# Modulation row sums issued beside the attention, single PSUM banks for the paired products, attention results fetched one load earlier, and program order kept on two engines in all pairs

## The chip, the cores and the metric

The kernel runs on one core of a Trainium2 chip. The metric is the device time of one execution in microseconds (us), lower is better. The program's instructions run on TensorE (PE), VectorE (DVE), ScalarE (ACT) and GpSimd (POOL); SyncE (SP) issues most of the transfers between HBM and the on-chip memory. Each engine works through its own instructions in the order in which they stand in its list, and waits for the others by semaphores.

## What is computed

One layer, in fp32, over 512 prompt tokens and 64 sample tokens (576 in all, width 1024): a modulation vector from the condition `c`, a normalised and modulated input, one wide projection, a gated causal convolution beside a sliding-window attention with sinks (16 heads of 64, 4 key heads, window 128), their gated mix, and then a gated feed-forward with its own causal convolution.

```python
mod = jax.nn.silu(c) @ w_ada + b_ada
sh1, sc1, g1, sh2, sc2, g2 = [m[:, None, :] for m in jnp.split(mod, 6, axis=-1)]
h = _rmsnorm(x, norm1_g) * (1.0 + sc1) + sh1
proj = h @ w_in
b_gate, c_gate, xa, q, k, v, ga, gb = jnp.split(proj, cuts, axis=-1)
uc, new_conv = _causal_conv(c_gate * xa, conv_buf, conv_w)
ya = (b_gate * uc) @ w_conv_out
o, k_state, v_state = attend(q, k, v, attn_sinks.reshape(N_KV_HEADS, GROUP))
yb = o @ w_attn_out
mixed = jax.nn.sigmoid(ga) * ya + jax.nn.sigmoid(gb) * yb
x = x + g1 * (mixed @ w_mix_out)
h2 = _rmsnorm(x, norm2_g) * (1.0 + sc2) + sh2
...
```

The sample tokens attend to cached keys and values. Of `mod`, columns 0 to 2047 (sh1, sc1) are needed at the start; columns 2048 to 6143 (g1, sh2, sc2, g2) only behind the attention. The outputs are both normalised token streams and the new convolution, key, value and feed-forward states.

## The kernel before

**Products.** An fp32 product is made from three matmul passes over operands split in a high and a low part (`whi`, `wlo` of a weight, `hh`, `hl` and the like of the input). The splits, made on ACT and DVE, are what these two engines mostly do. Two output blocks of 128 rows by 576 tokens are computed as a pair (`pair_product`) from seven part products of 288 columns instead of eight. A part is 12 matmuls into one of three PSUM banks X, Y and Z. The order is X, Z, Y, X, Y, Z, Y. Behind a part another engine reads its bank: ACT subtracts X into Y (behind part 1), copies Z to `p` (part 2) and subtracts Y into Z (part 3); DVE or the result's own function reads X (part 4), Y with `p` (part 5), Z with `p` (part 6) and Y (part 7).

**Banks.** PSUM has two pools here: `mm`, two tiles of 1024 columns, and `aux`, four banks of 512 that serve everything else in turn. In pairs 0 to 13 (`N_ATT` is 14) X and Y are in two `mm` tiles and Z in an `aux` bank; later X and Z are in `aux`, Y in `mm`.

**Jobs.** The wide projection and the convolution's output product run as 27 pairs, in the loop over `jobs` near the end of the kernel: gates, queries, convolution inputs and gates (0 to 22), then `w_conv_out` (23 to 26). Products with `w_attn_out`, `w_mix_out`, `w_up` and `w_down` follow.

**Work beside them.** A generator set by `fill` is stepped from `tick(2)`, once in each part behind its third matmul, at a rate of steps per tick. Beside the pairs it first yields the attention, 16 units of one key head and one block of 128 tokens. A unit's scores (`prompt_scores`), mask (`s<-V,aux`), maximum (`nmx`), exponentials, sums (`den`) and scaling are written out in one step; transposes (`prompt_turn`) and values (`prompt_values`) come in later steps. The decode steps follow, then `modulation(2048)`, which loads 32 tiles of 128 x 512 of `w_ada` (`ada`, 256 KB each, on SP's queue) and sums them in 8 calls of `side_by_side` (8 matmuls, 32 rows each, into four row groups of one bank). `modulation(4096)` is stepped beside the last job and the attn_out products.

**What sets the order.** A scheduler may move instructions, but not those issued through `pe`, `act`, `dve` and `pool` while they are in the list `pinned`: `keep_in_program_order` then puts such an instruction behind the one that was written out just before it on its engine. PE is pinned throughout; `act` and `dve` are added when pair 14 is reached. The attention's own ACT and DVE instructions are issued through `nc.scalar` and `nc.vector` and are not pinned themselves. Weight loads (`raw`, four buffers) and `ada` loads share SP's queue; a weight load waits there until its buffer is free.

**Attention results.** The outputs are written to `ot_dram`. `load_o` fetches them as `or` tiles and `part_o` splits them (`oh` first, on ACT) for the attn_out products: in the last job's steps two are loaded at step 0, and each `part_o(n)` loads up to `n + 2`.

Of the kernel before, what the change touches and what calls it, by code (L numbers as in the profile page):

```python
# [27 lines left out]
FCH = [(0, 8), (8, 22)]  # L28
FB = 14
LATE = 2  # L30
ROWS_AHEAD = 5
N_ATT = 14
Q_TICKS = 8
OPS_AT = 1, 2, 3, 4
CACHE_AT = 17
# [39 lines left out]
def step_kernel(ctx: ExitStack, tc: tile.TileContext, ins: dict, outs: list):  # L75
# [9 lines left out]

    cnt = [0]

    pm = ctx.enter_context(tc.tile_pool(name="pm", bufs=2, space=PSUM))
    pa = ctx.enter_context(tc.tile_pool(name="pa", bufs=4, space=PSUM))

    def nm(s):
        cnt[0] += 1
# [6 lines left out]
        return ap_.tile([P, 594], F32, tag="uy", name=nm(s), bufs=U_BUFS)  # L99

    def mmps():
        return pm.tile([P, 1024], F32, tag="mm", name=nm("mm"))

    def aux():
        return pa.tile([P, 512], F32, tag="aux", name=nm("aux"))
# [374 lines left out]
        order = {0: "sums1 ah al", 2: "bh bl sums2", 3: "dh dl", c_at: "ch cl"}  # L480
        return {at: (lambda names=names: [t[n]() for n in names.split()]) for at, names in order.items()}

    def pair_product(w, x, steps, out_a0, out_a1, out_b0, out_b1, apart=False, scale=1.0):

        X, Y = (halves(mmps())[1][:, :HT] if apart or n else aux()[:, :HT] for n in range(2))
        Z = aux()[:, :HT]
# [594 lines left out]
    def decode_values(q, s, cV):  # L1083
        pt = []
        for kt in range(2):
            a = aux()
            for hd in range(4):
                transpose(
                    a[:, hd * P : hd * P + P], s[hd // 2][:, hd % 2, kt * P : kt * P + P], ident
                )  # L1090
            t = slot("pt", shape=[P, 512])
            nc.scalar.copy(t, a)
            pt.append(t)
            yield False
        yield False
        c = slice(32 * q, 32 * q + 32)
        if not od:
            od.append(slot("od", shape=[P, NK, 64]))
        for j in range(2):
            O = aux()  # L1100
            parts = [(vt(4)[:, j * P : j * P + P], pt[1], slice(0, P))]
            for b in range(4):
                parts.append((cV[b // 2][:, b % 2, j * P : j * P + P], pt[0], slice(32 * b, 32 * b + 32)))
            for n, (v, x, r) in enumerate(parts):
                for hf in range(2):
                    at = (2 * j + hf) * P
                    matmul(
                        O[HALF[hf], r], v[:, HALF[hf]], x[:, at + r.start : at + r.stop],
                        start=n == 0, stop=n == 4,
                    )  # L1110
            oX = slot("oX", shape=[P, 2, 32])
            for hf in range(2):
                src = O[HALF[hf], :P].rearrange("p (b x g t) -> p x g b t", b=4, x=2, g=2)
                dst = od[0][:, 4 * j + 2 * hf : 4 * j + 2 * hf + 2, c]
                nc.scalar.copy(
                    dst[HALF[hf]].rearrange("p g (b t) -> p g b t", b=4), src[:, hf]
                )
                nc.scalar.copy(
                    oX[HALF[hf]].rearrange("p g (b t) -> p g b t", b=4), src[:, 1 - hf]
                )  # L1120
                nc.sync.dma_start(dst[HALF[1 - hf]], oX[HALF[hf]])
            yield False
# [58 lines left out]
                if i == 3:  # L1181
                    nc.scalar.dma_start(ot_dram[2 * hd + g], ot[2 * hd + g])

    def attention():
        units = [(hd, i) for hd in range(4) for i in range(4)]
        s, pts = {}, {}
        for n in range(len(units) + 3):
            if n == CACHE_AT:
                cache_load(0)
            if n < len(units):  # L1190
                hd, i = units[n]
                while 2 * hd + 1 not in QS or ticks[0] < ready[hd]:
                    yield False
                s[n] = prompt_scores(hd, i)
            if n >= 4 and n % 2 == 0:
                prompt_values([(*units[u], pts.pop(u)) for u in (n - 4, n - 3)])
            yield False
            if 2 <= n <= len(units) + 1:
                pts[n - 2] = prompt_turn(units[n - 2][1], s.pop(n - 2))
            yield False  # L1200
        filler[1] = .45
        before = None
        for n in range(3):
            s, more = [], []
            if n < 2:
                yield from decode_scores(n, s, more)
            if before is not None:
                yield from before
            before = decode_values(n, s, more)
# [52 lines left out]
    def side_by_side(ps, ks, cols):  # L1262
# [2 lines left out]
        order = [(k, j) for k in reversed(ks) for j in (3, 0, 1, 2)]  # L1265
        for n, (k, j) in enumerate(order):
            done = nc.tensor.matmul(  # L1267
                ps[32 * j : 32 * j + 32, :], cT[:, k, :], cols[k][j],
                start=(k == 1), stop=(k == NK - 2),
            )  # L1270
            if n:
                tc.keep_in_program_order(done)

    def modulation(c0):

        ps = aux()
        cols = [[None] * 4 for _ in range(NK)]
        for n in range(4 * NK + ROWS_AHEAD):
            if n < 4 * NK:
                k, j = n // 4, n % 4  # L1280
                cols[k][j] = slot("ada", shape=[P, 512])
                c = c0 + 512 * j
                nc.sync.dma_start(cols[k][j], ins["w_ada"][0, k * P : k * P + P, c : c + 512])
            yield False
            done = n + 1 - ROWS_AHEAD
            if done > 0 and done % 8 == 0:
                side_by_side(ps, (done // 4 - 2, done // 4 - 1), cols)
                yield False
        row = slot("row", shape=[P, 512])
        nc.scalar.copy(row, ps)  # L1290
        yield False
        t = aux()
        yield False
        for cc in range(4):
            transpose(t[:, cc * P : cc * P + P], row[:, cc * P : cc * P + P], ident)
        b0 = c0 // P
        nc.vector.tensor_tensor(
            out=modT[:, b0 : b0 + 16, :].rearrange("p (j c) r -> p j c r", j=4),
            in0=t.rearrange("p (c j r) -> p j c r", c=4, j=4)[:, :, :, 0:9],
            in1=parT[:, b0 : b0 + 16]  # L1300
            .rearrange("p (j c) -> p j c", j=4)
            .unsqueeze(3)
            .to_broadcast([P, 4, 4, 9]),
            op=ALU.add,
        )
        yield False

    def modulations(n):
        yield from modulation((2048, 4096)[n])
        yield True  # L1310

    def beside_conv():
        yield from attention()
        filler[1] = 40 / 84
        yield from modulation(2048)
        yield True

    fill(beside_conv(), .28)
# [214 lines left out]
    for n in range(4):  # L1533
        if n:
            jobs[n_conv + n].before = {
                1: [lambda n=n: late[2 * n - 2]()], 2: [lambda n=n: late[2 * n - 1]()],
            }
    jobs[-1].after = {
        0: [lambda: load_o(2)], 2: [lambda: part_o(2)], 3: [lambda: part_o(3)],
        4: [lambda: w_next.update({1: split_w(w_raw)})], 5: [lambda: part_o(4)], 6: [lambda: part_o(6)],  # L1540
        7: [lambda: part_o(8)],
    }
# [9 lines left out]
    def part_o(n):  # L1552
        for k in range(len(o), n):
            o.append(split_slot(o_raw[k], "o"))
        load_o(min(n + 2, NK))

    for n, job in enumerate(jobs):
        if n == N_ATT:
            pinned += [act, dve]
        if n + 1 == len(jobs):  # L1560
            drain()
            fill(modulations(1), 0.6)
        if n + 2 < len(jobs):
            jobs[n + 2].load()
        elif n + 2 > len(jobs):
# [5 lines left out]
        pair_product(job.w, job.ops["op"], joined(job.before, steps, job.after), *outs, n < N_ATT, job.scale)  # L1571
# [701 lines left out]
```

## Time and profile before

| | |
|---|---|
| time, median of 3 runs | 974.13 us (972.2 to 977.55) |
| the profiled execution | 974.38 us |
| its span, first to last instruction | 972.6 us |
| mean granted PE clock | 0.991 |
| POOL busy | 142.5 us (15%) |
| HBM traffic over the span | 134 GB/s |

In rows of the profile a line such as `PE L117 MATMUL aux<-t,whi` names the engine, the line of the kernel (often that of the helper that issues all pinned instructions: 117 in before, 136 in the changed kernel), the operation, and the tile written and the ones read. `x2` counts instructions that are merged in one row. In brackets stands the idle time ahead of the instruction and what ended it. Busy time of PE counts its matmuls. The pairs run from about 73 us on; the attention's units lie between 74 and 270 us, the modulations between 339 and 470 us.

### The profile page before, as it was taken

How to read it: one execution, taken by the hardware profiler on the slowest of the kernel's cores; microseconds unless marked ns; L12 is line 12 of the kernel's file. 1: busy time of each engine (PE TensorE's matmuls, PEld its weight loads, DVE VectorE, ACT ScalarE, POOL GpSimd, SP SyncE). 2: the span in 40 equal slices, each digit the busy share in tenths (PEclk: the TensorE clock that was granted, in tenths of full speed). 3: DMA queues.
4: the chain of work that ended last, by engine and by line, in shares of the span. 5: the costliest groups of instructions: out<-in, count | busy, mean ns of one | idle time of the engine just before them, and what ended most of it. 6: DMA issues, size and time to landing. Idle time of an engine off the chain costs nothing.

```text
span 972.6 us, 18634 instructions
## 1 busy us (share of the span) xinstructions
PE 944.0 (97%) x7218; PEld 900.2 (93%) x7218; DVE 723.5 (74%) x1366; ACT 572.3 (59%) x1086; POOL 142.5 (15%) x320
## 2 busy tenths in 40 slices
PE   7999999999999999897999999999999999999997
PEld 6798989988999989797899999999999999999997
DVE  5687987879586676665677678995558998868874
ACT  5366777767667656675445657564226655546664
POOL 2221111022121222111000121100000000001110
PEclk9999999999999999898999999999999999999999
DMA  9976466544565999789895742233333333327542
GB/s 287 315 219 178 113 197 170 158 110 110 157 167 137 235 254 275 206 223 280 271 280 163 170 116 73 66 108 88 86 89 96 99 88 87 104 65 175 136 95 98
DMA packets 186442, 154.30 MB, mean 159 GB/s; under 512 B 7896, under 2 KB 162332, under 8 KB 186066
## 3 DMA queue, kind: packets, MB, share of 16 engines
q1 hardware_dynamic: 173698, 113.81, 39.1%
q0 software_dynamic: 11360, 36.94, 17.5%
q10 hardware_dynamic: 1296, 2.36, 0.7%
q8 instruction: 56, 0.92, 0.4%
q14 instruction: 32, 0.26, 0.1%
HBM read 115.98 MB, written 14.17 MB: 134 GB/s over the span
## 4 chain that ended last, share of the span: by engine, by line
PE 82%; DMA 7%; ACT 5%; DVE 2%; issue 2%; SPq 1%; POOL 0%; ACTq 0%; DVEq 0%; POOLq 0%
PE mm L117 46%; PE aux L117 34%; DMA ada<-in_w_ada 2%; PE aux L1267 2%; ACT whi L117 1%; DMA ad<-in_w_ada 1%; DMA wlo<-raw 1%; PE aux L1169 1%; DMA or<-ot_dram 1%; ACT s L1009 1%; DMA raw<-in_w_in 1%; DMA raw<-in_w_down 1%; ACT wlo L117 1%; SPq L531 1%; DMA out<-so 0%
## 5 line engine op out<-in xcount | busy, mean ns | idle before, releaser
L117 ACT ACTIVATE whi<-raw 128x1024 fp32r<-128x1024 f32 (+3 forms) x192 | 194.7, 1023 | 112.1 <-PE aux L117 35.4
L117 DVE TENSOR_TENSOR wlo<-raw,whi 128x1024 fp32r<-128x1024 f32 (+3 forms) x153 | 180.2, 1184 | 29.8 <-ACT whi L117 29.5
L117 DVE TENSOR_TENSOR raw<-raw 128x512 f32<-128x512 f32 x100 | 70.1, 701 | 2.4
L117 PE MATMUL aux<-2h,whi 128*128 128x288 f32 (+2 forms) x232 | 68.7, 296 | 0.0
L117 PE MATMUL aux<-2h,wlo 128*128 128x288 f32 (+2 forms) x232 | 68.5, 295 | 0.0
L117 PE MATMUL aux<-2l,whi 128*128 128x288 f32 (+2 forms) x232 | 68.5, 295 | 0.0
L117 POOL DMA_DIRECT2D wlo<-raw x39 | 34.4, 881 | 184.4 <-ACT wlo L117 69.8
L117 PE MATMUL aux<-hh,whi 128*128 128x288 f32 (+2 forms) x180 | 53.2, 303 | 0.0
L117 PE MATMUL aux<-hh,wlo 128*128 128x288 f32 (+2 forms) x180 | 51.9, 295 | 0.0
L117 PE MATMUL aux<-hl,whi 128*128 128x288 f32 (+2 forms) x180 | 51.8, 295 | 0.0
L117 PE MATMUL mm<-fh,whi 128*128 128x256 f32 x224 | 47.8, 295 | 0.3 <-DVE rt L117 0.3
L117 PE MATMUL mm<-fh,wlo 128*128 128x256 f32 x224 | 47.7, 295 | 0.0
L117 PE MATMUL mm<-fl,whi 128*128 128x256 f32 x224 | 47.1, 292 | 0.0
L117 PE MATMUL mm<-hh,whi 128*128 128x288 f32 (+2 forms) x160 | 45.3, 307 | 0.5 <-ACT hh L117 0.5
L117 PEld LDWEIGHTS aux<-2h,whi 128*128 128x128 f32 x232 | 43.6, 188 | 0.0
L117 PEld LDWEIGHTS aux<-2l,whi 128*128 128x128 f32 x232 | 43.6, 188 | 0.0
L117 PEld LDWEIGHTS aux<-2h,wlo 128*128 128x128 f32 x232 | 43.6, 188 | 0.0
L117 DVE SCALAR_TENSOR_TENSOR y<-pad,par2T,y 128x592 f32<-128x592 f32 x44 | 36.6, 833 | 9.0 <-ACT y L117 8.2
L117 PE MATMUL mm<-hh,wlo 128*128 128x288 f32 (+2 forms) x160 | 43.2, 295 | 0.0
L117 PE MATMUL mm<-hl,whi 128*128 128x288 f32 (+2 forms) x160 | 42.5, 297 | 0.0
L117 PE MATMUL mm<-t,whi 128*128 128x288 f32 x184 | 39.6, 306 | 2.6 <-ACT mm L117 2.6
L117 ACT ACTIVATE wlo<-whi 128x1024 fp32r<-128x1024 f32 (+1 forms) x39 | 40.0, 1025 | 0.8
(392 smaller groups left out, 3237.9 us busy)
## 6 DMA issues: line engine op xcount, KB each, us to landing
raw<-in_w_in SPq DMA_DIRECT2D x52, 512.0 KB, 4.6
raw<-in_w_up SPq DMA_DIRECT2D x44, 512.0 KB, 3.9
wlo<-raw POOLq DMA_DIRECT2D x33, 512.0 KB, 4.8
ada<-in_w_ada SPq DMA_DIRECT2D x64, 256.0 KB, 5.6
ad<-in_w_ada SPq DMA_DIRECT2D x32, 256.0 KB, 6.6
raw<-in_w_down SPq DMA_DIRECT2D x16, 512.0 KB, 4.1
sg_dram<-sg POOLq DMA_DIRECT2D x16, 288.0 KB, 3.9
gt<-sg_dram SPq DMA_DIRECT2D x16, 288.0 KB, 5.5
```

The source lines that it names most:

```text
L117: done = getattr(self.engine, name)(*args, **kwargs)
L531: return tc.keep_in_program_order(nc.sync.dma_start(dst, src))
L1009: nc.scalar.activation(s[x // 2][:, x % 2, :w], s[x // 2][:, x % 2, :w], AF.Exp, bias=nmx[:, x : x + 1], accum_out=den[:, x : x + 1],)
L1169: done = nc.tensor.matmul(O[HALF[par], c], vt(i - nkt + 1 + kt)[:, hd * 64 : hd * 64 + 64], pts[kt][:, par * 256 : par * 256 + 256], start ...
L1267: done = nc.tensor.matmul(ps[32 * j : 32 * j + 32, :], cT[:, k, :], cols[k][j], start=(k == 1), stop=(k == NK - 2),)
```

## The change

1. A class `Modulations` takes the place of the generator. It covers the same columns of `w_ada` in four groups of 1024 (2048, 3072, 4096, 5120), with 64 tiles of 128 x 2 x 256 (two row blocks, 256 KB each). Loads are issued one or two per step of the attention's generator, at most 7 ahead of the sums (`MOD_AHEAD`); a call of 8 matmuls of 256 columns sums four of them, at the earliest 6 ticks after the last was issued (`MOD_TICKS`), beside the attention's values, and after the attention at a rate of 0.3. There are 16 calls in place of 8.
2. While the jobs run, PSUM is divided into four single banks `bx`, `by`, `bz` (X, Y and Z of every pair), `rows` (the modulation sums) and the four of `aux`. Then the two `mm` tiles come back.
3. `act` and `dve` are pinned from pair 0 (`N_SET`) and not from pair 14.
4. Three `or` tiles are loaded already in the last job but one, and `part_o(n)` loads up to `n + 3`.

```diff
-ROWS_AHEAD = 5
+MOD_AHEAD = 7
+MOD_TICKS = 6
 N_ATT = 14
+N_SET = 0
...
+    def banks(**pools):
+
+        sums["stack"] = ExitStack()
+        for name, (n, cols) in pools.items():
+            pool = sums["stack"].enter_context(
+                tc.tile_pool(name=name + str(cnt[0]), bufs=n, space=PSUM)
+            )
+            sums[name] = lambda pool=pool, cols=cols, name=name: pool.tile(
+                [P, cols], F32, tag=name, name=nm(name)
+            )
+
+    banks(mm=(2, 1024))
+    ctx.callback(lambda: sums.pop("stack").close())
...
+    def pair_product(w, x, steps, out_a0, out_a1, out_b0, out_b1, scale=1.0):
+        if "bx" in sums:
+            X, Y, Z = (sums[n]()[:, :HT] for n in ("bx", "by", "bz"))
+        else:
+            X, Y = (halves(mmps())[1][:, :HT] if n else aux()[:, :HT] for n in range(2))
+            Z = aux()[:, :HT]
...
+            mods.sums()
...
+                sums()
...
-                ps[32 * j : 32 * j + 32, :], cT[:, k, :], cols[k][j],
+                ps[32 * j : 32 * j + 32, :], cT[:, k, :], cols[j][:, k % 2, :],
...
-    def modulation(c0):
-        for n in range(4 * NK + ROWS_AHEAD):
-            if n < 4 * NK:
-                k, j = n // 4, n % 4
-                cols[k][j] = slot("ada", shape=[P, 512])
-                c = c0 + 512 * j
-                nc.sync.dma_start(cols[k][j], ins["w_ada"][0, k * P : k * P + P, c : c + 512])
+    class Modulations:
+        def __init__(self, firsts):
+            self.todo = [(c0, kp, j) for c0 in firsts for kp in range(4) for j in range(4)]
+            self.cols, self.rows = [], None
+
+        def load(self, n=1):
+            for _ in range(n):
+                if not self.todo or len(self.cols) >= MOD_AHEAD:
+                    return
+                c0, kp, j = self.todo.pop(0)
+                t = slot("ada", shape=[P, 2, 256])
+                c = c0 + 256 * j
+                src = ins["w_ada"][0, 2 * kp * P : 2 * kp * P + 2 * P, c : c + 256]
+                nc.sync.dma_start(t, src.rearrange("(k p) m -> p k m", p=P))
+                self.cols.append((t, kp, c0, ticks[0]))
+
+        def sums(self):
+
+            if self.rows and self.rows[1] + 2 <= ticks[0]:
+                self.turn()
+            if len(self.cols) < 4 or ticks[0] < self.cols[3][3] + MOD_TICKS:
+                return
+            cols, self.cols = self.cols[:4], self.cols[4:]
+            kp, c0 = cols[0][1:3]
+            if kp == 0:
+                self.ps = sums["rows"]()
+            side_by_side(self.ps[:, :256], (2 * kp, 2 * kp + 1), [x[0] for x in cols])
...
+    mods = Modulations((2048, 3072, 4096, 5120))
+
+    def beside_conv():
+        for n, _ in enumerate(attention(mods.sums)):
+            mods.load(1 + n % 2)
...
-    def beside_conv():
-        yield from attention()
-        filler[1] = 40 / 84
-        yield from modulation(2048)
+        filler[1] = .3
+        while mods.left():
+            mods.load()
+            yield False
+            mods.sums()
...
+    jobs[-2].after = {5: [lambda: load_o(3)]}
     jobs[-1].after = {
-        0: [lambda: load_o(2)], 2: [lambda: part_o(2)], 3: [lambda: part_o(3)],
+        2: [lambda: part_o(2)], 3: [lambda: part_o(3)],
...
-        load_o(min(n + 2, NK))
-
+        load_o(min(n + 3, NK))
+    banks(bx=(1, 512), by=(1, 512), bz=(1, 512), rows=(1, 512))
-        if n == N_ATT:
+        if n == N_SET:
             pinned += [act, dve]
-            fill(modulations(1), 0.6)
...
+    banks(mm=(2, 1024))
```

`q_909` and `q_910` are the two query blocks of pair 1, `q_913` and `q_914` those of pair 7; `s` are scores of an attention unit, `raw`, `wlo` and `wl` belong to the weights of the next pairs. The first place is DVE in pair 1, before:

```order
L1137 SCALAR_TENSOR_TENSOR s_1267<-V_686,aux_1269 128x256
L1137 SCALAR_TENSOR_TENSOR s_1268<-V_686,aux_1269 128x256
L117 TENSOR_TENSOR s_1336<-raw_1139,raw_1141 128x512
L1137 SCALAR_TENSOR_TENSOR s_1267<-V_686,aux_1270 128x256
L1137 SCALAR_TENSOR_TENSOR s_1268<-V_686,aux_1270 128x256
L117 TENSOR_TENSOR raw_1141<-raw_1141 128x512
L117 SCALAR_TENSOR_TENSOR q_909<-aux_1145,p_1146 128x288
L1000 TENSOR_REDUCE nmx_1279<-s_1267 128x2
L1000 TENSOR_REDUCE nmx_1279<-s_1268 128x2
L117 TENSOR_TENSOR wlo_1340<-raw_1139,whi_1339 128x1024
```

and in the changed kernel, where the Z bank is `bz` and the unit has `s_1294` and `s_1295`:

```order
L1160 SCALAR_TENSOR_TENSOR s_1294<-V_686,aux_1297 128x256
L1160 SCALAR_TENSOR_TENSOR s_1295<-V_686,aux_1297 128x256
L136 TENSOR_TENSOR raw_1168<-raw_1168 128x512
L1022 TENSOR_REDUCE nmx_1306<-s_1294 128x2
L1022 TENSOR_REDUCE nmx_1306<-s_1295 128x2
L1025 TENSOR_TENSOR nmx_1306<-nmx_1306,nsnk 128x4
L1028 TENSOR_TENSOR es_1311<-snk,nmx_1306 128x4
L1038 TENSOR_TENSOR den_1310<-den_1310,es_1311 128x4
L1039 RECIPROCAL den_1310<-den_1310 128x4
L1041 TENSOR_SCALAR s_1294<-s_1294,den_1310 128x256 x2
L1041 TENSOR_SCALAR s_1295<-s_1295,den_1310 128x256 x2
L136 SCALAR_TENSOR_TENSOR q_909<-bz_1172,p_1173 128x288
```

The read of Z (`q_909<-aux` before, `q_909<-bz` now) stood ahead of the maximum; now it stands behind the maximum, the two small sums and the last scaling; a `wlo` stands between the two pairs of masks, one row ahead of the first one shown. The second place is DVE in pair 7, before:

```order
L1137 SCALAR_TENSOR_TENSOR s_2470<-V_686,aux_2472 128x256
L1137 SCALAR_TENSOR_TENSOR s_2471<-V_686,aux_2472 128x256
L1137 SCALAR_TENSOR_TENSOR s_2470<-V_686,aux_2473 128x256
L1137 SCALAR_TENSOR_TENSOR s_2471<-V_686,aux_2473 128x256
L1000 TENSOR_REDUCE nmx_2482<-s_2470 128x2
L117 SCALAR_TENSOR_TENSOR q_914<-mm_2339,p_2341 128x288
L1000 TENSOR_REDUCE nmx_2482<-s_2471 128x2
```

and now (Y is `by`):

```order
L1160 SCALAR_TENSOR_TENSOR s_2562<-V_686,aux_2565 128x256
L1160 SCALAR_TENSOR_TENSOR s_2563<-V_686,aux_2565 128x256
L1022 TENSOR_REDUCE nmx_2574<-s_2562 128x2
L1022 TENSOR_REDUCE nmx_2574<-s_2563 128x2
L1025 TENSOR_TENSOR nmx_2574<-nmx_2574,nsnk 128x4
L1028 TENSOR_TENSOR es_2579<-snk,nmx_2574 128x4
L1038 TENSOR_TENSOR den_2578<-den_2578,es_2579 128x4
L1039 RECIPROCAL den_2578<-den_2578 128x4
L1041 TENSOR_SCALAR s_2562<-s_2562,den_2578 128x256 x2
L1041 TENSOR_SCALAR s_2563<-s_2563,den_2578 128x256 x2
L136 SCALAR_TENSOR_TENSOR q_914<-by_2415,p_2417 128x288
L136 TENSOR_TENSOR wlo_2557<-raw_2167,whi_2556 128x1024
```

The read of Y behind part 5 stood between the two maxima; now it stands behind the last scaling. The third place is PE at the start of pair 0, before:

```order
L117 MATMUL mm_919<-hh_593,wlo_888 128x320
L117 MATMUL aux_1000<-ident,st_682 128x128
L117 MATMUL aux_1003<-ident,par_902 128x74
L117 MATMUL mm_1012<-hh_344,whi_923 128x288
L117 MATMUL mm_1012<-hl_345,whi_923 128x288
```

and now:

```order
L136 MATMUL mm_919<-hh_593,wlo_888 128x320
L136 MATMUL aux_1006<-ident,st_682 128x128
L1291 MATMUL rows_1640<-ada_1063,cT 32x256
L1291 MATMUL rows_1640<-ada_955,cT 32x256
L1291 MATMUL rows_1640<-ada_991,cT 32x256
L1291 MATMUL rows_1640<-ada_993,cT 32x256
L1291 MATMUL rows_1640<-ada_1063,cT 32x256
L1291 MATMUL rows_1640<-ada_955,cT 32x256
L1291 MATMUL rows_1640<-ada_991,cT 32x256
L1291 MATMUL rows_1640<-ada_993,cT 32x256
L136 MATMUL aux_1009<-ident,par_902 128x74
L136 MATMUL bx_1031<-hh_344,whi_923 128x288
```

The eight matmuls of the first modulation sums stand ahead of pair 0's first product (`mm_1012` before, `bx_1031` now); on SP their loads `ada_955`, `ada_991` and `ada_993` stand ahead of the weight load `raw_1025`, and `ada_1063` behind it.

More of the change, by code (lines that the diff above doesn't have):

```diff
@@ L86, in step_kernel @@
     cnt = [0]
-    pm = ctx.enter_context(tc.tile_pool(name="pm", bufs=2, space=PSUM))
     pa = ctx.enter_context(tc.tile_pool(name="pa", bufs=4, space=PSUM))
+    sums = {}
+    def banks(**pools):
+        if sums:
+            sums.pop("stack").close()
+            sums.clear()
+        sums["stack"] = ExitStack()
[8 more added lines that the diff above has]
+    ctx.callback(lambda: sums.pop("stack").close())
     def nm(s):
@@ L101, in mmps @@
     def mmps():
-        return pm.tile([P, 1024], F32, tag="mm", name=nm("mm"))
+        return sums["mm"]()
     def aux():
@@ L481, in in_turn @@
         return {at: (lambda names=names: [t[n]() for n in names.split()]) for at, names in order.items()}
-    def pair_product(w, x, steps, out_a0, out_a1, out_b0, out_b1, apart=False, scale=1.0):
-        X, Y = (halves(mmps())[1][:, :HT] if apart or n else aux()[:, :HT] for n in range(2))
-        Z = aux()[:, :HT]
+    def pair_product(w, x, steps, out_a0, out_a1, out_b0, out_b1, scale=1.0):
[4 more added lines that the diff above has]
+            Z = aux()[:, :HT]
         p5 = slot("p5")[:, :HT]
@@ L1182, in prompt_values, with attention @@
                     nc.scalar.dma_start(ot_dram[2 * hd + g], ot[2 * hd + g])
-    def attention():
+    def attention(sums):
         units = [(hd, i) for hd in range(4) for i in range(4)]
@@ L1272, in side_by_side @@
                 tc.keep_in_program_order(done)
-    def modulation(c0):
-        ps = aux()
-        cols = [[None] * 4 for _ in range(NK)]
-        for n in range(4 * NK + ROWS_AHEAD):
-            if n < 4 * NK:
-                k, j = n // 4, n % 4
-                cols[k][j] = slot("ada", shape=[P, 512])
-                c = c0 + 512 * j
-                nc.sync.dma_start(cols[k][j], ins["w_ada"][0, k * P : k * P + P, c : c + 512])
-            yield False
[L1285 to L1306, printed above, removed]
@@ L1308, in modulations, with turn, left @@
-    def modulations(n):
-        yield from modulation((2048, 4096)[n])
-        yield True
-    def beside_conv():
-        yield from attention()
-        filler[1] = 40 / 84
-        yield from modulation(2048)
+    class Modulations:
[22 more added lines that the diff above has]
+            side_by_side(self.ps[:, :256], (2 * kp, 2 * kp + 1), [x[0] for x in cols])
+            if kp == 3:
+                if self.rows:
+                    self.turn()
+                row = slot("row", shape=[P, 256])
+                nc.scalar.copy(row, self.ps[:, :256])
+                self.rows = row, ticks[0], c0
+        def turn(self):
+            (row, _, c0), self.rows = self.rows, None
+            t = aux()
+            for cc in range(2):
+                transpose(t[:, cc * P : cc * P + P], row[:, cc * P : cc * P + P], ident)
+            b0 = c0 // P
+            nc.vector.tensor_tensor(
+                out=modT[:, b0 : b0 + 8, :].rearrange("p (j c) r -> p j c r", j=4),
+                in0=t[:, :256].rearrange("p (c j r) -> p j c r", c=2, j=4)[:, :, :, 0:9],
+                in1=parT[:, b0 : b0 + 8]
+                .rearrange("p (j c) -> p j c", j=4)
+                .unsqueeze(3)
+                .to_broadcast([P, 4, 2, 9]),
+                op=ALU.add,
+            )
+        def left(self):
+            return bool(self.todo or self.cols or self.rows)
@@ L1570, in step_kernel @@
         outs = job.outs()
-        pair_product(job.w, job.ops["op"], joined(job.before, steps, job.after), *outs, n < N_ATT, job.scale)
+        pair_product(job.w, job.ops["op"], joined(job.before, steps, job.after), *outs, job.scale)
+    banks(mm=(2, 1024))
     mixed, raw_mx, made_m = [None] * NK, [None] * NK, {}
```

## The prediction

> **What bounds the kernel now.** I read the page's first part and its chain, then the waits of TensorE (PE), then the timeline around its longest idle times, then busy time by stage.
>
> ```profile
> PE 944.0 (97%) x7218; PEld 900.2 (93%) x7218; DVE 723.5 (74%) x1366; ACT 572.3 (59%) x1086; POOL 142.5 (15%) x320
> ...
> PE 82%; DMA 7%; ACT 5%; DVE 2%; issue 2%; SPq 1%; POOL 0%; ACTq 0%; DVEq 0%; POOLq 0%
> ```
>
> PE is busy 97% of 972.6 us and carries 82% of the chain that ended last. The change barely alters what PE computes, so I look only for PE's idle time: what goes, and what comes.
>
> ```profile
> PE aux L1267 <- DMA ada<-in_w_ada: 5.2, 2, 3.7
> PE mm L117 <- DVE ya L117: 4.9, 1, 4.9
> PE aux L117 <- POOL ident masks.py:199: 4.5, 1, 4.5
> PE mm L117 <- ACT mm L117: 2.6, 2, 1.8
> PE mm L117 <- ACT aux L117: 2.5, 4, 0.9
> ```
>
> Columns: waiting engine and tile, who released it; us in total, times, longest. The third row is the start of the kernel and stays. The two ada waits are modulation loads after the attention; the ya wait belongs to the first attn_out product; the two ACT rows, 5.1 us, are PE waiting for ScalarE to empty a bank beside the attention (but one small one).
>
> ```profile
> 357.29 1.07 PE L1267 MATMUL aux<-ada,cT 128*32 128x512 f32 x8 [1.46 <-DMA ada<-in_w_ada]
> 395.76 3.64 PE L1267 MATMUL aux<-ada,cT 128*32 128x512 f32 x16 [3.73 <-DMA ada<-in_w_ada]
> 458.53 0.61 PE L117 MATMUL mm<-nh,whi 128*128 128x288 f32 x1 [4.95 <-DVE ya L117]
> ...
> 454.93 0.68 ACT L117 ACTIVATE oh<-or 128x576 fp32r<-128x576 f32 x1 [4.84 <-DMA or<-ot_dram]
> ...
> 451.60 6.37 DMA or<-ot_dram
> ```
>
> These are the places: PE stands 1.46, 3.73 and 4.95 us (brackets: idle ahead of the instruction, and its releaser). Behind the last wait the chain is a fetched attention result `or` that took 6.37 us; ScalarE's split of it waited 4.84 us, and PE's next operand queued behind that.
>
> ```profile
> 118.00:270.00 152.00, 149.80 (x1150) 136.90 (x1146) 119.31 (x289) 107.23 (x272) 27.43 (x40) 1.00 0.56 150
> 340.00:405.00 65.00, 59.82 (x434) 52.25 (x427) 41.29 (x66) 35.83 (x59) 14.03 (x22) 0.95 0.90 250
> 405.00:470.00 65.00, 59.08 (x426) 57.39 (x425) 41.26 (x61) 42.81 (x71) 9.12 (x16) 0.95 0.91 260
> 394.35:401.17 6.82, 5.41 (x23) 2.43 (x24) 3.66 (x7) 2.52 (x3) 0.88 (x1) 0.50 0.74 182
> 455.79:462.61 6.82, 4.08 (x17) 4.08 (x18) 4.66 (x7) 3.52 (x6) 0.00 (x0) 0.50 0.95 319
> ```
>
> Windows: length, busy time of PE, PEld, DVE, ACT, POOL, PE's granted clock, DMA share, GB/s. Beside the attention (first row) PE is full, DVE 78% and ACT 71% busy. The next two stages have DMA at 0.90. The last two rows show a second price of a stall: around the idles of 3.73 and 4.95 us PE's clock stood at 0.50 for 6.82 us. The busy time in them, 5.41 and 4.08 us, ran at half speed and so lost up to 2.7 and 2.0 us. The 1.46 us idle left no such mark.
>
> [...]
>
> **The change, part by part.** Durations come from one profiled execution of 974.38 us, 0.25 above the median of the three runs shown (974.13); the sum is made against the 974.38.
>
> *What goes.* (a) The modulation loads are issued beside the attention, where DMA stands at 0.56, and not in the stages at 0.90; so 1.46 + 3.73 and the first half-clock stretch, 2.7, should go: 7.9. (b) `or` is fetched one load further ahead; 4.95 and 2.0 should go: 7.0. I take 13.5 of the 14.9, since the last fetches still share a busy queue; bounds 8 (all of b stays) to 15. (c) ScalarE's and VectorE's reads of a product are now held in program order from the first pair, so the 5.1 us of ACT waits beside the attention go, but for some 0.4 outside it: 4.7, between 2 and 5.
>
> *What comes: softmax ahead of the bank reads.* One attention unit is written out whole (scores, mask, max, exps, sums, scaling) at one place of the program. In before, VectorE's read of a product bank may pass that softmax; now it stands behind the last scaling, as the order rows above show for `q<-bz` and `q<-by`. An engine works through its rows in order, so VectorE can't read the bank until ScalarE's exps have ended, and Z has one bank where before it had one of four. In before the same unit went like this:
>
> ```profile
> 96.50 0.38 PE L117 MATMUL aux<-kX,q 64*128 64x256 f32 x1
> 96.81 0.40 PE L117 MATMUL aux<-hh,whi 128*128 128x288 f32 x1
> ...
> 98.10 0.29 PE L117 MATMUL mm<-n4h,whi 128*128 128x288 f32 x1
> ...
> 99.70 0.29 PE L117 MATMUL mm<-hh,whi 128*128 128x288 f32 x1
> ...
> 101.30 0.42 PE L117 MATMUL aux<-t,whi 128*128 128x288 f32 x2
> ```
>
> ```profile
> 96.91 0.75 DVE L1137 SCALAR_TENSOR_TENSOR s<-V,aux 128x256 f32<-128x256 f32 x2
> 97.58 0.68 DVE L117 TENSOR_TENSOR s<-raw,raw 128x512 f32<-128x512 f32 x1
> ...
> 99.44 0.45 DVE L117 SCALAR_TENSOR_TENSOR q<-aux,p 128x288 f32<-128x288 f32 x1
> 99.81 1.27 DVE L1000 TENSOR_REDUCE nmx<-s 128x2 f32<-128x512 f32 x2
> 101.00 1.21 DVE L117 TENSOR_TENSOR wlo<-raw,whi 128x1024 fp32r<-128x1024 f32 x1
> 102.56 0.16 DVE L1003 TENSOR_TENSOR nmx<-nmx,nsnk 128x4 f32<-128x4 f32 x1
> ...
> 105.25 0.15 DVE L1016 TENSOR_TENSOR den<-den,es 128x4 f32<-128x4 f32 x1
> ```
>
> ```profile
> 102.76 0.51 ACT L1009 ACTIVATE s<-s,nmx 128x256 f32<-128x256 f32 x1 [0.39 <-DVE nmx L1003]
> ...
> 104.75 0.19 ACT L1015 ACTIVATE es<-es 128x4 f32<-128x4 f32 x1
> ```
>
> ```profile
> L1019 DVE TENSOR_SCALAR s<-s,den 128x256 f32<-128x256 f32 x40 | 11.4, 350 | 0.2
> ```
>
> Scores end at 96.9. Part 6 ends at 98.1, part 7 at 99.7 (a part is 1.60 us), part 1 of the next pair at 101.3, and there part 2 needs Z. In before `q<-aux` ran at 99.44, ahead of the max. In the new order VectorE has to do, from 96.9: two mask pairs 1.5, `s<-raw,raw` and one more like it 1.36, `wlo` 1.21, the max 1.27, the small minimum 0.16: 5.5, so to 102.4, or 101.9 with starts packed as before's (0.07 each under the duration). Exps and `es` take ScalarE 2.2 (102.76 to 104.94), then `den` and its reciprocal 0.3, four scalings at 11.4/40 = 0.285 each 1.15, `q<-bz` 0.45: 106.0 where PE wants it at 101.3. **Wait: 4.7 us.** Without the `wlo` it is 3.5; with the two weight additions gone also, 2.3. The pair in which the unit falls decides which. Four units (pairs 1 to 4, counting from 0) have their scores in part 6: 4 x 3.75 = 15.
>
> Three units (pairs 7, 9, 10) have them in part 5, before Y is read for part 7: 1.3 us of part 5 and 1.6 of part 6 are the whole cover, 2.9 us; in pair 7 eight transposes lie between, some 1.1 more. The chain without weight work is 1.4 + 1.2 + 0.1 + 2.2 + 0.3 + 1.15 + 0.45 = 6.8. Waits of 3.9, 3.9 and 2.8: 10.6. Behind PE's waiting instruction stands everything else of PE, so these are on the path.
>
> ScalarE's own reads of Y and Z (the subtractions) now stand behind the four exps where a unit falls in part 1 or 2: up to 2.2 us each, but half of it is covered by the part that runs; I take 3 in all (0 to 5).
>
> Together 28.6. Lower bound: 4 x 2.3 less a cover of VectorE being ahead by 1 us each, 3 x 2.8, nothing for ScalarE: 14. Upper: 4 x 4.7 + 3 x (3.9 + 1.21) + 5 = 39.
>
> *Half clock after them.* The idles of 3.73 and 4.95 us halved the clock, 1.46 did not. Of the seven waits three are near 4 or above: 3 x 2.0 = 6; bounds 0 and 7 x 2.0 = 14.
>
> *The first sums.* Its four loads stand in SyncE's queue among weight loads and the sums stand on PE ahead of pair 0's first matmul:
>
> ```profile
> 72.58 4.40 SPq L156 DMA_DIRECT2D raw<-in_w_in  x2
> ...
> 78.30 0.53 PE L117 MATMUL mm<-t,whi 128*128 128x288 f32 x2 [1.85 <-ACT mm L117]
> ...
> ada<-in_w_ada SPq DMA_DIRECT2D x64, 256.0 KB, 5.6
> ```
>
> The last of the four is behind the weight load of 72.58; with that landed in 3.8 or so it is there near 76 or 77, where PE arrives at 73: 2.5 after giving back part of the 1.85 counted under (c); 0 to 4.5. Elsewhere a sums call comes six steps after its last load; a load that stands behind a weight load held by its buffer can still be late: 2 in all, 0 to 5.
>
> *More pieces.* A call of 8 matmuls over 512 columns becomes two over 256, and these are issued in 21 pieces where before had 8:
>
> ```profile
> 339.32 1.92 PE L1267 MATMUL aux<-ada,cT 128*32 128x512 f32 x16
> ```
>
> Half such a call took 1.07 at 357.29 where 0.96 is half of 1.92, so 0.11 for each of 13 more pieces: 1.5. The transposes and additions of four rows replace those of two double ones, hidden beside PE's other work or alike. POOL's and SyncE's instruction counts don't change.
>
> **Sum:** 28.6 + 6 + 2.5 + 2 + 1.5 - 13.5 - 4.7 = +22.4; 974.4 + 22.4 = 997 us.
>
> **Rivals.** *1, faster:* the reads don't hold PE. Then -13.5 - 4.7 + 1.5 + 2 = -14.7, 960 us. It needs a softmax that ends within the cover, 4.4 us (part 6) or 2.9 (part 5), after the scores. Against it: exps, scalings and the read alone are 2.2 + 1.15 + 0.45, and masks and max add 2.6. For it: only that VectorE may use PE's waits to be ahead. *2, about even:* the waits are at their low bound, no clock is lost, the loads are in time: 14 + 1.5 + 2.5 - 18.2 = -0.2, 974 us. *3, worse:* every wait halves the clock and `or` stays late: 28.6 + 14 + 6 - 8 - 4.7 = +36, 1010 us. *4, the change doesn't do what it says:* loads only trade places, because one SyncE queue carries weights and modulations, and the waits for ada appear beside the attention: +7 on the forecast, 1004 us.
>
> **How the numbers follow.** Forecast with its neighbours 3 and 4: 0.55, 0.12, 0.11; rival 1: 0.12; rival 2: 0.10. The range leaves out the best part of rival 1 and the far side of 3: 971 to 1015. Faster by over 0.5% (under 969.3; 0.5% is about what a measurement of this kernel can tell from no change): rival 1 and a little of 2, 0.14. Within: 0.08. Slower: 0.78.
>
> **What would show it.** In the changed profile: rows of PE waiting for DVE's `q` on bz and by in the attention, 3 to 5 us long, seven of them; a granted clock under 1.00 between 74 and 270 where it is 1.00 now; no ada wait after the attention; no 4.9 us wait for ya. The forecast is wrong if PE stays full between 118 and 270, or if the max and the exps end before part 7 does.

## The result and the profile after

The changed kernel takes 1014.83 us (median of 4 runs, 1013.48 to 1017.02) where the kernel before, on the same chip, takes 973.62: a ratio of 1.0419 (95% interval 1.0383 to 1.0455), slower by 41 us. The forecast was 997 us in a range of 971 to 1015: the side and the mechanism came out, but the loss was nearly twice the 22 us forecast, and the time lies only 0.2 us inside the range.

The page of the changed kernel, its first line, PE's clock in 40 slices, and the chain that ended last:

```profile
PE 962.3 (95%) x7346; PEld 914.4 (90%) x7346; DVE 729.1 (72%) x1368; ACT 573.2 (57%) x1088; POOL 135.8 (13%) x320
...
PEclk9999889999989999999999999999999999999999
...
PE 80%; DVE 8%; ACT 6%; DMA 4%; issue 2%; SPq 0%; ACTq 0%; DVEq 0%
```

The span grew from 972.6 to 1011.5 us. PE's busy time rose by 18.3 us, though its work is nearly the same, and its idle time (span less busy) by 20.6. VectorE's share of the chain went from 2% to 8%. PE's waits of the changed kernel:

```profile
PE bz L136 <- DVE q L136: 8.3, 2, 4.8
PE by L136 <- DVE g L136: 6.7, 3, 5.5
PE aux L136 <- POOL ident masks.py:199: 4.5, 1, 4.5
PE by L136 <- DVE x L136: 4.4, 1, 4.4
PE bz L136 <- DVE sg L136: 4.2, 2, 3.9
PE rows L1291 <- DMA ada<-in_w_ada: 3.6, 2, 3.4
PE by L136 <- DVE q L136: 3.4, 1, 3.4
PE by L136 <- DVE sg L136: 2.3, 1, 2.3
PE by L136 <- ACT bz L136: 1.6, 3, 1.0
```

The waits for the modulations after the attention and for `ya` (10.1 us) have gone, but for 0.2 us, and new ones for VectorE's reads of the banks `bz` and `by` have come: 8.3 + 6.7 + 4.4 + 4.2 + 3.4 + 2.3 = 29.3 us. The first of the long ones, at part 2 of pair 2, in the timelines of PE, DVE and ACT:

```profile
106.42 0.29 PE L136 MATMUL bx<-hh,wlo 128*128 128x288 f32 x1
111.52 0.85 PE L136 MATMUL bz<-t,whi 128*128 128x288 f32 x2 [4.80 <-DVE q L136]
```

```profile
105.84 1.27 DVE L1022 TENSOR_REDUCE nmx<-s 128x2 f32<-128x512 f32 x2
107.14 0.16 DVE L1025 TENSOR_TENSOR nmx<-nmx,nsnk 128x4 f32<-128x4 f32 x1
107.34 0.16 DVE L1028 TENSOR_TENSOR es<-snk,nmx 128x4 f32<-128x4 f32 x1
109.54 0.16 DVE L1038 TENSOR_TENSOR den<-den,es 128x4 f32<-128x4 f32 x1 [2.04 <-ACT es L1037]
109.74 0.18 DVE L1039 RECIPROCAL den<-den 128x4 f32<-128x4 f32 x1
109.95 1.14 DVE L1041 TENSOR_SCALAR s<-s,den 128x256 f32<-128x256 f32 x4
111.01 0.45 DVE L136 SCALAR_TENSOR_TENSOR q<-bz,p 128x288 f32<-128x288 f32 x1
```

```profile
107.34 0.51 ACT L1031 ACTIVATE s<-s,nmx 128x256 f32<-128x256 f32 x1 [4.91 <-DVE nmx L1025]
...
109.32 0.19 ACT L1037 ACTIVATE es<-es 128x4 f32<-128x4 f32 x1
```

Read it backwards. PE starts on Z at 111.52, when `q<-bz` has read it (111.01 to 111.46). That read was possible long before, since PE's last matmul into Z ended at 103.5; it stood behind four scalings, these behind `den`, and ahead of `den` VectorE stood idle for 2.04 us until ScalarE had finished the exponentials. All three engines wait for each other in turn, and the two that hold PE are not full: DVE 72%, ACT 57%.

The second loss is in the windows of half clock. Of the eight between 74 and 300 us, three, then the sum of all eight, and the last 60 us of that time as a whole:

```profile
108.88:115.71 6.83, 4.19 (x16) 3.09 (x17) 4.34 (x14) 4.19 (x9) 2.21 (x3) 0.50 0.03 5
207.87:211.28 3.41, 3.41 (x16) 3.14 (x16) 2.23 (x4) 1.02 (x2) 0.89 (x2) 0.50 0.45 125
289.79:296.62 6.83, 5.89 (x25) 5.88 (x26) 4.19 (x9) 2.13 (x3) 1.03 (x2) 0.50 0.42 125
...
sum 37.55, PE 33.67 PEld 29.37 DVE 21.72 ACT 18.20 POOL 10.41; mean PE 4.21 PEld 3.67 DVE 2.71 ACT 2.27 POOL 1.30
...
240.00:300.00 60.00, 50.06 (x360) 43.69 (x360) 41.68 (x96) 30.61 (x76) 4.85 (x14) 0.91 0.51 141
```

Each long wait has 3.41 or 6.83 us at 0.50 at its end or behind it, even the wait of 2.27 us ahead of 207.37. The eight hold 33.67 us of PE's busy time. How much of it was lost can be read from the starts of one kind of matmul, first at full clock, then in the window from 207.87, where PE is busy throughout:

```profile
203.99 0.30 PE L136 MATMUL bz<-hh,whi 128*128 128x288 f32 x1
204.12 0.30 PE L136 MATMUL bz<-hl,whi 128*128 128x288 f32 x1
...
208.11 0.44 PE L136 MATMUL by<-n4l,whi 128*128 128x288 f32 x1
208.35 0.44 PE L136 MATMUL by<-n4h,wlo 128*128 128x288 f32 x1
```

They start 0.13 us apart at 1.00 and 0.24 us apart at 0.50, so a window at half clock does 0.13 / 0.24, a little over half, of the work. An estimate from these rows for all eight: 33.67 x (1 - 0.13 / 0.24), some 15 us lost, and 16.8 if it were a full half.

### The profile page after: what moved, and what is told of

Same layout as the page of the kernel before. It is cut to its first block, busy times and chain, and to the rows that moved or that the text cites. A ratio compares the mean times of both kernels' runs of the same rounds, so it can differ in the third digit from the quotient of the medians.

```text
span 1011.5 us, 18885 instructions
## 1 busy us (share of the span) xinstructions
PE 962.3 (95%) x7346; PEld 914.4 (90%) x7346; DVE 729.1 (72%) x1368; ACT 573.2 (57%) x1088; POOL 135.8 (13%) x320
## 4 chain that ended last, share of the span: by engine, by line
PE 80%; DVE 8%; ACT 6%; DMA 4%; issue 2%; SPq 0%; ACTq 0%; DVEq 0%
PE mm L136 32%; PE aux L136 22%; PE by L136 11%; PE bz L136 7%; PE bx L136 6%; ACT s L1031 2%; DMA ad<-in_w_ada 1%; DVE s L1160 1%; PE rows L1291 1%; DVE nmx L1022 1%; DMA ada<-in_w_ada 1%; PE aux L1192 1%; DVE raw L136 1%; DVE s L1041 1%; DVE wlo L136 1%
## 5 line engine op out<-in xcount | busy, mean ns | idle before, releaser
L136 PE MATMUL bx<-hh,whi 128*128 128x288 f32 x184 | 57.3, 311 | 0.0
L136 PE MATMUL bx<-hl,whi 128*128 128x288 f32 x184 | 55.7, 303 | 0.0
L136 PE MATMUL bx<-hh,wlo 128*128 128x288 f32 x184 | 55.3, 300 | 0.0
L136 PE MATMUL bz<-t,whi 128*128 128x288 f32 x184 | 41.7, 319 | 12.6 <-DVE q L136 8.3
L1031 ACT ACTIVATE s<-s,nmx 128x256 f32<-128x256 f32 (+1 forms) x72 | 33.9, 474 | 26.7 <-DVE nmx L1025 26.7
L136 PEld LDWEIGHTS bz<-t,whi 128*128 128x128 f32 x184 | 31.5, 203 | 17.0 <-DVE q L136 8.8
L136 PE MATMUL by<-n4h,whi 128*128 128x288 f32 x92 | 30.7, 333 | 16.8 <-DVE g L136 6.7
```

The source lines that it names most:

```text
L136: done = getattr(self.engine, name)(*args, **kwargs)
L1031: nc.scalar.activation(s[x // 2][:, x % 2, :w], s[x // 2][:, x % 2, :w], AF.Exp, bias=nmx[:, x : x + 1], accum_out=den[:, x : x + 1],)
```

## The experiments

Each time is a median, and each ratio is to the kernel before, timed on the same chip (975.3 to 975.8 us).

**1. Undo the pinning alone.**

```diff
-N_SET = 0
+N_SET = 14
```

> The changed kernel with N_SET back at 14: VectorE and ScalarE are pinned from pair 14 on, all else as changed. Theory 'softmax ahead of the reads': the waits of PE for VectorE's reads of by and bz (29.3 us in the changed kernel's profile) and most of the half-clock time that follows them (some 15 us) go, so about 968 us; up to 975 if the 5.1 us of waits for ScalarE come back. Rival 'single banks': X, Y and Z in one bank each hold PE whatever the order, so it stays above 995 us.

Measured: 965.68 us, ratio 0.9902 (0.9875 to 0.9930). The single banks, the modulations beside the attention and the early fetches are all still there, and the kernel is faster than both. Page and timeline of this kernel, at the same read:

```profile
PE 944.1 (98%) x7346; PEld 900.2 (93%) x7346; DVE 723.9 (75%) x1368; ACT 572.1 (59%) x1088; POOL 141.4 (15%) x320
```

```profile
99.12 0.68 DVE L136 TENSOR_TENSOR raw<-raw 128x512 f32<-128x512 f32 x1
99.72 0.45 DVE L136 SCALAR_TENSOR_TENSOR q<-bz,p 128x288 f32<-128x288 f32 x1
100.09 1.27 DVE L1022 TENSOR_REDUCE nmx<-s 128x2 f32<-128x512 f32 x2
```

The read stands ahead of the maximum and is done at 100.17; PE takes Z at 101.59 without a wait. Its mean granted clock is 0.998 over 963.5 us, so that at most some 5 us of it were at 0.50, where the changed kernel's 0.979 over 1011.5 us makes some 42. Pinning from pair 0 thus costs some 49 us (1014.83 against 965.68), and the spans, 48.0 us apart, split it: PE busy 962.3 against 944.1, 18.2 us, and idle 49.2 against 19.4, 29.8 us. The rival 'single banks' falls.

**2. The pinning alone, in the kernel before.**

```diff
-        if n == N_ATT:
+        if n == 0:
             pinned += [act, dve]
```

> The kernel before with VectorE and ScalarE pinned from pair 0, nothing else. Theory 'order and single bank together': where the late read is of Y (parts 5 and 4: 16.5 us of waits in the changed kernel) it holds PE here too, where it is of Z (12.7 us) it does not, since Z is one of four aux banks; with half clock of some 8 us and the 5.1 us of waits for ScalarE gone, about 993 us. Rival 'order alone': all seven waits, 1010 us or more. Rival 'banks alone': no change, 974 us.

Measured: 1018.30 us, ratio 1.0429 (1.0390 to 1.0468). My expectation of 993 missed, and the rival 'order alone' came out. The waits of PE in this kernel:

```profile
PE mm L117 <- ACT mm L117: 6.7, 4, 2.2
PE mm L117 <- DVE g L117: 5.9, 2, 5.4
...
PE mm L117 <- DVE x L117: 4.8, 1, 4.8
...
PE mm L117 <- DVE sg L117: 3.7, 2, 3.5
PE mm L117 <- DVE q L117: 3.4, 1, 3.4
PE mm L117 <- ACT aux L117: 3.0, 5, 1.0
PE aux L1169 <- DVE sg L117: 2.8, 1, 2.8
```

The waits for reads of Y are there (5.9 + 4.8 + 3.7 + 3.4). Those for Z are not, as I had worked out, but others stand in their place: four for ScalarE's subtractions into the `mm` banks (6.7 us, 2.6 before) and one of 2.8 us of the attention's values for an aux bank. The order is enough to slow the kernel; more banks for Z only move the wait.

**3. A second bank for Z in the changed kernel.**

```diff
-    pa = ctx.enter_context(tc.tile_pool(name="pa", bufs=4, space=PSUM))
+    pa = ctx.enter_context(tc.tile_pool(name="pa", bufs=3, space=PSUM))
...
-    banks(bx=(1, 512), by=(1, 512), bz=(1, 512), rows=(1, 512))
+    banks(bx=(1, 512), by=(1, 512), bz=(2, 512), rows=(1, 512))
```

> The changed kernel with two banks for Z and three for aux in place of one and four. Theory 'order and single bank together': the waits at part 2 of pairs 2, 3, 4 and 5 (12.5 us) and the half clock behind them (about 8 us) go, those at part 7 (16.5 us) stay: about 994 us. Rival 'ScalarE or VectorE is simply full': the work queues up and PE waits for it elsewhere, no gain; and if three aux banks are too few, waits for aux banks appear in the profile instead.

Measured: 1002.70 us, ratio 1.0271 (1.0234 to 1.0309): 12 us of some 20 expected. In its profile

```profile
PE by L136 <- DVE g L136: 6.7, 3, 5.5
...
PE by L136 <- ACT by L136: 4.4, 3, 2.3
```

the waits on `bz` for VectorE (12.5 us) are gone and those on `by` are as long as ever; but 4.4 us of waits for ScalarE's subtractions into Y have come, as in experiment 2. The bank was taken from `aux`, where 2.1 us of new waits for ScalarE stand, so this run tries two things at once.

**4. Idle matmuls in place of PE's idle time.** The wait stays, PE works on nothing of use.

```diff
+            if (pair_no[0], at) in FILL:
+                keep_warm(aux(), FILL[pair_no[0], at])
             part(bank, wn, xn_, at > 1)
```

> The changed kernel with idle matmuls of 128x128 (0.108 us each, into an aux bank that nobody reads) written ahead of the parts at which PE waits: 40, 31, 28 ahead of part 2 in pairs 2, 3, 5, and 18, 27, 36, 46 ahead of part 7 in pairs 6, 7, 9, 10, a little less than each wait lasted. The waits end when they did, but PE is not idle. Theory 'half clock': the clock stays at 1.00 there and some 15 us lost at 0.50 come back, about 999 us. Rival 'the clock has other reasons, or what is saved is waited for behind it': within 3 us of the changed kernel's 1014.

Measured: 1021.25 us, ratio 1.0467 (1.0444 to 1.0491). This run missed its purpose: an idle matmul was two passes of 0.11 us (the first block, of 40, has 80 rows in 9.09 us), so the blocks lasted up to 10 us and went on for 1 to 5 us after the reads they covered. It tells nothing on its question. The next run has half as many.

> As filled2, with about half as many idle matmuls (21, 17, 15 and 11, 15, 19, 24), since each took 0.22 us there and not 0.11, so that the seven blocks lasted past the reads they stand in for. Theory 'half clock': with blocks as long as the waits, PE at full clock does the work behind them sooner, 998 to 1004 us. Rival 'what is saved is waited for behind it': 1010 us or more.

Measured: 1003.61 us, ratio 1.0294 (1.0275 to 1.0314). Windows of PE around the first wait, changed kernel, then this one:

```profile
105.00:112.00 7.00, 2.20 (x15) 1.97 (x15) 4.82 (x14) 4.66 (x13) 0.00 (x0) 0.78 0.25 75
```

```profile
105.00:112.00 7.00, 6.89 (x56) 6.16 (x56) 4.46 (x15) 5.74 (x14) 1.21 (x2) 1.00 0.08 25
```

PE's clock is 1.00 there and from 264 to 275 and 288 to 296 us, where the last two waits lay, and its mean of 0.998 over 1000.9 us leaves at most some 5 us at 0.50 in the whole execution; VectorE and ScalarE are as busy over the whole span (729.0 and 572.8 us against 729.1 and 573.2), and the kernel is 11 us faster with 122 useless matmuls more. How these 11 us go with the 15 estimated above is in two rows of this kernel, PE's share and the idle matmuls (with 14 others that take 2.0 us in the changed kernel):

```profile
PE 974.8 (97%) x7590; PEld 928.1 (93%) x7590; DVE 729.0 (73%) x1368; ACT 572.8 (57%) x1088; POOL 135.2 (14%) x320
...
L138 PE MATMUL aux<-ident 128*128 128x128 f32 x258 | 30.4, 275 | 0.0
```

Without the idle matmuls, 28.4 us, PE is busy for 946.4 us, 15.9 less than the 962.3 of the changed kernel. But PE's idle time fell by only 23.1 (49.2 to 26.1) for these 28.4, so 5.3 us were given back. The half clock thus took about 15 us of PE's time, and 11 us of them show in the kernel's time here.

**5. Which engine's order.**

```diff
         if n == N_SET:
-            pinned += [act, dve]
+            pinned += [dve]
+        if n == N_ATT:
+            pinned += [act]
```

> The changed kernel with VectorE pinned from pair 0 and ScalarE only from pair 14. Theory 'VectorE's read stands behind the last scaling': nearly all of the loss stays, 1005 us or more, with the waits for q, x, g and sg on by and bz as long as they were. Rival 'ScalarE's order is what makes the softmax late': less than half of the loss stays, under 990 us.

Measured: 1014.74 us, ratio 1.0408 (1.0385 to 1.0431). VectorE's order alone is the whole loss. With `act` and `dve` exchanged:

> The changed kernel with ScalarE pinned from pair 0 and VectorE only from pair 14; VectorE's reads stand ahead of the maximum again. Theory 'VectorE's read stands behind the last scaling': the seven long waits are gone; only ScalarE's own reads behind the exponentials are left, some 1 to 2 us each in three or four pairs: 968 to 975 us. Rival 'ScalarE's order': over 990 us.

Measured: 979.27 us, ratio 1.0047 (1.0025 to 1.0068). The long waits are gone, but it is 14 us above experiment 1 and 4 above what I expected. PE's waits here:

```profile
PE by L136 <- ACT by L136: 4.5, 2, 3.0
PE rows L1291 <- DMA ada<-in_w_ada: 3.3, 1, 3.3
PE by L136 <- ACT bz L136: 2.9, 3, 1.0
```

PE waits 7.4 us for ScalarE's own reads, where experiment 1 has 1.9 and the forecast had 3, and the first modulation sums wait 3.3 us. The two costs do not add: with VectorE pinned, pinning ScalarE as well changed nothing (1014.83 against 1014.74).

**6. The end of the softmax written one step later**, pinned from pair 0 as in the changed kernel.

```diff
-        softmax(ss, 4, snk[:, 4 * hd : 4 * hd + 4], nsnk[:, 4 * hd : 4 * hd + 4], w)
-        return ss
+        tail = softmax_steps(ss, 4, snk[:, 4 * hd : 4 * hd + 4], nsnk[:, 4 * hd : 4 * hd + 4], w)
+        for _ in range(3):
+            next(tail)
+        return ss, tail
...
             yield False
+            if n < len(units):
+                for _ in tail:
+                    pass
```

> The changed kernel, pinned from pair 0, with the end of each prompt unit's softmax (sum with the sink, reciprocal, four scalings) written out one step of the generator later, behind the reads that it stood ahead of. Theory 'VectorE stands for ScalarE's exponentials ahead of the read': each read comes some 3.7 us sooner, the waits for VectorE fall from 29.3 us to under 10, hardly any half clock is left, and the time is near that with only ScalarE pinned early (979 us): 976 to 986 us. Rival 'program order as such costs, wherever the softmax stands': over 1000 us.

Measured: 986.62 us, ratio 1.0117 (1.0101 to 1.0134), 28 us faster than the changed kernel and just above the upper end of what was expected (986). DVE and PE at the same read:

```profile
106.39 0.16 DVE L1025 TENSOR_TENSOR nmx<-nmx,nsnk 128x4 f32<-128x4 f32 x1
106.58 0.16 DVE L1028 TENSOR_TENSOR es<-snk,nmx 128x4 f32<-128x4 f32 x1
106.66 0.46 DVE L136 SCALAR_TENSOR_TENSOR q<-bz,p 128x288 f32<-128x288 f32 x1
```

```profile
105.67 0.29 PE L136 MATMUL bx<-hh,wlo 128*128 128x288 f32 x1
107.18 0.53 PE L136 MATMUL bz<-t,whi 128*128 128x288 f32 x2 [1.21 <-DVE q L136]
```

The read comes right behind the maximum, 1.0 us after PE's last matmul on X (105.67 to 106.66) where it came 4.6 us after it (106.42 to 111.01), and the wait is 1.21 us where it was 4.80. The pinning is as in the changed kernel, so most of its cost is not program order as such, but what the program writes ahead of the read. Not all has gone: 21 us are left over experiment 1. The profile has 8.0 us of waits for VectorE's reads (0.7 there), 7.0 for ScalarE's (1.9) and 3.4 for the first sums (0.6); PE is busy for 949.7 us (944.1), and its mean granted clock is 0.996 (0.998).

**7. The banks alone, in the kernel before** (pinned from pair 14, `rows` unused).

```diff
+    banks(bx=(1, 512), by=(1, 512), bz=(1, 512), rows=(1, 512))
     for n, job in enumerate(jobs):
...
-        X, Y = (halves(mmps())[1][:, :HT] if apart or n else aux()[:, :HT] for n in range(2))
-        Z = aux()[:, :HT]
+        if "bx" in sums:
+            X, Y, Z = (sums[n]()[:, :HT] for n in ("bx", "by", "bz"))
...
```

> The kernel before with the new banks alone (bx, by, bz and an unused fourth while the jobs run), pinned from pair 14, modulations and fetches as before. The forecast put the end of the waits for ScalarE beside the attention (5.1 us) down to the pinning; they are gone without it, so theory 'the banks end them': 969 us, the rest as before. Rival 'the modulations end them, by moving what VectorE and ScalarE do': 974 us with the waits of before; and if single banks cost something, more than 974.

Measured: 975.03 us, ratio 0.9998 (0.9986 to 1.0010). The banks cost and bring nothing that can be told; PE still waits 4.3 us for ScalarE (2.4 on `bz`, 1.9 on `by`).

**8. The fetches alone.** In the kernel before:

```diff
+    jobs[-2].after = {5: [lambda: load_o(3)]}
...
-        load_o(min(n + 2, NK))
+        load_o(min(n + 3, NK))
```

> The kernel before with the attention results fetched earlier (three loads in the last job but one, then up to n + 3) and nothing else. Theory 'the fetch is what ya waits behind': the 4.95 us wait goes with its 2 us of half clock, about 968 us. Rival 'the queue is full there, only the modulations' leaving it makes room': the wait stays or moves to a weight load, 972 us or more.

Measured: 973.71 us, ratio 0.9987 (0.9971 to 1.0002): no difference that can be told. The wait for `ya` is gone, but a third wait for a modulation stands behind it (timeline of PE):

```profile
466.08 1.92 PE L1267 MATMUL aux<-ada,cT 128*32 128x512 f32 x4 [1.82 <-DMA ada<-in_w_ada]
```

And taken out of experiment 1:

> The changed kernel pinned from pair 14 with the fetches of the attention results as before (two loads at step 0 of the last job, then up to n + 2). Theory 'the fetch is what ya waits behind': a wait of some 5 us and half clock return, about 972 us. Rival 'the modulations' leaving the queue is enough': as with the early fetch, 966 us.

Measured: 970.88 us, ratio 0.9952 (0.9936 to 0.9968), 5.2 us more than with the early fetches. There PE waits again:

```profile
461.98 0.40 PE L136 MATMUL by<-nh,whi 128*128 128x288 f32 x1 [3.27 <-DVE ya L136]
```

So the early fetch brings 5 us once the modulations have left the queue, and nothing that can be told while they are in it.

## Why the forecast was right in kind and short in size

- **Softmax ahead of the reads: right, its size partly by luck.** Forecast 28.6 us of waits, measured 29.3 for VectorE and 1.6 for ScalarE. At the worked example the forecast had 4.7 us and the trace 4.80, with the same rows behind one another. By place: on `bz` in pairs 2 to 5 12.5 us (forecast 15), on `by` in pairs 7, 9 and 10 3.4 + 4.4 + 5.5 = 13.3 (10.6). These are not quite the seven that were forecast: pair 4, with 3.75 us in the forecast, waited 0.4, and pair 6, not in the forecast, 2.3, so the sum is nearer than its terms. Experiments 1, 5 and 6 show the cause: it is VectorE's order, and within it mostly the tail of the softmax (28 of 49 us).
- **Half clock: the term that was mis-sized.** "Of the seven waits three are near 4 or above: 3 x 2.0 = 6." All seven and the first sums' wait were followed by a stretch at 0.50, three of them by 6.83 us. The measured cost is some 15 us of PE's time, of which experiment 4 got 11 back. That only waits near 4 us would have one was my estimate from the two idles in the trace of before, 3.73 and 4.95 us; the shortest wait that had one here was 2.27 us.
- **First sums: right in kind.** Forecast 2.5 us, measured 3.4 us of wait and a stretch of 3.41 us at 0.50 (78.16 to 81.58). It, too, hangs on the pinning: experiment 1 waits 0.6 us at this place, and there the fourth load stands ahead of the weight load on SyncE.
- **What goes: too much was counted.** Without the late reads the forecast made 960 us (rival 1); experiment 1, which is that case, is 965.7. The waits did go. But PE's busy time there is 944.1 us, as in the kernel before, although up to 4.7 us of half-clock loss are gone. The sums in smaller pieces, mis-sized too, make up for most of it: their matmuls take 19.6 us there and 17.3 in the kernel before, of which 1.7 is half clock (3.64 against 1.92 for the same sixteen), so up to 4.0 more where the forecast had 1.5. The 4.0 can hold some overlap with other matmuls.
- **A wrong reason.** The forecast put the end of the ACT waits beside the attention down to the pinning. Pinning ScalarE adds such waits (7.4 us in experiment 5, 1.9 in experiment 1), the banks alone leave 4.3 of 5.1, and only kernels with the moved modulations have few (1.9 in experiment 1, 1.6 in the changed kernel). That the modulations shift what ScalarE does at these places is likely, but was not tried by itself.
- **The rivals.** A decision point was named, a softmax that ends within 4.4 or 2.9 us after the scores; in the changed kernel it took about 9 from the end of the scores in pair 1. Rival 4, ada waits beside the attention, is 3.6 us and no more.
- **The sum.** By spans the loss against experiment 1 is 18.2 us of busy and 29.8 of idle time. Of the 18.2, some 15 are the half clock in the eight windows; up to 1.7 more can be a stretch of 3.41 us ahead of the pairs, which the changed kernel's execution has (from 16.72), as that of the kernel before (from 15.47); experiment 1's mean clock of 0.998 does not tell whether it has one. Of the idle time 29.3 less the 0.7 that experiment 1 has too is the reads. That the time came to lie 0.2 us inside the range is luck: the half clock, at some 15 us, is at or above even the upper bound of its own term (14), and the pieces had no bound.

## What to carry to other kernels

Before pinning an engine to the program's order, look at what the program writes ahead of the short instruction that frees a bank: a chain that crosses to another engine and back can hold it while both engines have idle time. Here the read came 4.6 us after PE's last matmul on X, with VectorE busy for 72% and ScalarE for 57% of the span. Split such a chain where it crosses, and put the part that waits behind the reads. And count the clock beside the wait: here PE's slow stretches cost some 11 to 15 us on top of 33 us of waits.

## What was not expected of the hardware

But for the one at the very end of each execution, the half clock came in stretches of 3.41 or 6.83 us: one and two of them in the trace of the kernel before, six and three in that of the changed kernel. The length of the idle time alone did not tell which would have one. In the kernel before, 1.67 us ahead of a matmul at 15.37 had 3.41 us at 0.50 from 15.47 on, and 1.85 us ahead of one at 78.30 had none (1.00 from 74 to 118 us). In the changed kernel 2.27 us had one; in the last run 3.27 us had none (1.00 from 440 to 490 us). Beside and behind the attention the two idles of 3.73 and 4.95 us in the kernel before and the seven of 3.39 to 5.50 us in the changed one all had one. In the changed kernel the same matmul of 288 columns took 0.44 us at 0.50 where it took 0.30 at 1.00, and started 0.24 us behind the one before it where it started 0.13.
